# A hybrid attention and mixture-of-experts block on one core: the large weights are laid out by the host in blocks of 1 MiB, 8 KiB per partition

## The chip, the cores and the metric

The kernel runs on one core of one Trainium2 chip. The metric is the device time of one execution in microseconds (us), lower is better. The kernel before took 781.64 us as the median of three runs (780.91 to 783.07). Arithmetic that the host does on its side before the launch (sorting an input into another order in memory) is not part of this time; what the device reads and computes is.

## The reference

One decoder block over 256 tokens of 1024 channels, in float32. Two token mixers work on the same normed input, are gated, merged and projected; then each token goes to two of 32 experts.

```python
h = rmsnorm(x, g_mix); proj = h @ w_in            # w_in: 1024 x 7936
q_d, k_d, v_d, q_s, k_s, v_s, gate_d, gate_s = split_cols(proj, IN_WIDTHS)
y_dil = dilated_attention(q_d, k_d, v_d)          # 24 heads, three dilations
y_swa = swa_sink_attention(q_s, k_s, v_s, sinks)  # 16 query heads on 2 key heads
mixed = sigmoid(gate_d) * (y_dil @ w_br_dil) + sigmoid(gate_s) * (y_swa @ w_br_swa)
x = x + mixed @ w_out
# hier_moe(rmsnorm(x, g_ffn)): the best of 4 groups, the two best of its 8 experts
for e in range(32):
    a = silu(hf @ w_e_gate[e]) * (hf @ w_e_up[e])  # 1024 x 512 each
    out = out + gates[:, e:e + 1] * (a @ w_e_down[e])  # 512 x 1024
x = rmsnorm(x + out, g_final)
```

The weights are far larger than the data: w_in, w_br_dil, w_br_swa and w_out hold 43 MB, the three expert weights 32 x 6 MiB = 201 MB. All of them are read once.

## The kernel before

The work has two stages that overlap at their seam.

*The mixers* (to about 310 us). `Stream` (L153 to L172) brings the dense weights in tiles `w` of 128 partitions x 4 row blocks x 512 columns, 1 MiB each, in the order of the list `items`; four tiles rotate. A tile is asked for with one transfer, whose source is cut out of the weight matrix as it stands: for each partition four pieces of 512 neighbouring float32 (2 KiB), one from each of four rows of the matrix. `convert` (L232) splits each tile into two parts of lower precision with ScalarE (L248) and VectorE (L249), and TensorE multiplies both. A tile's slot is free for the next one once both engines have read it.

*The experts*. All 32 experts are computed for the tokens that chose them, 32 slots per expert. Their weights come in 192 chunks `ew` of 1 MiB, six per expert: four of gate and up (256 input rows each), two of down (256 hidden rows each). `fill` (L643) asks for them: a chunk of gate and up with two transfers of 512 KiB (one from `w_e_gate`, one from `w_e_up`), in which a partition gets two neighbouring rows of 512 float32 (4 KiB, in one piece); a chunk of down with one transfer of 1 MiB, two pieces of 4 KiB per partition from rows 128 apart. Chunks go into a ring of slots, which grows whenever the mixers give up a buffer (`release`); `prefetch` asks for the next chunk as soon as the program has come to a place where one is called for, and the chunk's slot has been read by TensorE. Per expert TensorE gathers tokens (`ga`, for four experts at a time), multiplies by gate and up (`gu`), turns the activation (`atp`), multiplies by down (`dn`) and adds into four accumulators (`quad`).

Nearly all transfers are issued by one queue, SyncE's (SP), in program order: a transfer whose slot is not free holds back all that stand behind it. The framework also gives each transfer one of eight completion semaphores in turn (DMAHW0 to DMAHW7 in the rows of the order below), and a transfer waits until the one that had the semaphore before has landed. So at most eight are under way.

The rows of an input channel and its place: in the gate and up chunks partition p holds rows 2p and 2p+1 of 256, so the transposes of x2 (`xtp`, L127 called from `route_piece`) and the gathers (`ga`) read x2 with a step of two elements; the router weights `wr` and the norm's gains `fcol` are stored the same way.

```python
src[(k0 + j) * P:(k0 + j + step) * P, c0:c0 + ncol].rearrange("(k p) c -> p k c", p=P),  # L170, dense tile
src[e, 256 * i:256 * (i + 1), :].rearrange("(p r) c -> p (r c)", r=2))                   # L648, gate or up
w_e_down[e, 256 * i + rows * j:256 * i + rows * (j + 1), :].rearrange("(c p) o -> p c o", p=P))  # L655, down
```

Of the kernel before, what the change touches and what calls it, by code (L numbers as in the profile page):

```python
# [9 lines left out]
F32 = mybir.dt.float32  # L10
# [74 lines left out]
def tile_hybrid_block(  # L85
    ctx: ExitStack,
    tc: tile.TileContext,
    x, g_mix, w_in, sinks, w_br_dil, w_br_swa, w_out, g_ffn, w_group, b_group,
    w_router, b_router, w_e_gate, w_e_up, w_e_down, g_final, c_small, c_big, out,
):  # L90
    nc = tc.nc
    x, w_in, out = x[0], w_in[0], out[0]
    w_br_dil, w_br_swa, w_out = w_br_dil[0], w_br_swa[0], w_out[0]
    w_group, w_router = w_group[0], w_router[0]
    w_e_gate, w_e_up, w_e_down = w_e_gate[0], w_e_up[0], w_e_down[0]
# [14 lines left out]
    # x and the output come with the tokens by their class, the token modulo 4, and in order within it:  # L110
    # place 64 c + j is token 4 j + c.
# [19 lines left out]
    # ---------------------------------------------------------------- loads  # L131
# [4 lines left out]
    frow = sb.tile([4, 2 * P], F32, tag="ct0", name="frow")  # L136
# [17 lines left out]
    class Stream:  # L154
        """Dense weights, 512 columns by 4 row blocks of 128, in the order they are used."""
# [4 lines left out]
        def load(self):  # L160
            if self.n >= len(self.items):
                return
            src, k0, nk, c0, ncol = self.items[self.n]
            s = self.free.pop(0)
            t = slot(s, [P, 4, 512], f"w{self.n}")
            step = 2 if self.n == 0 else nk
            for j in range(0, nk, step):
                SP.dma_start(
                    t[:, j:j + step, :ncol],
                    src[(k0 + j) * P:(k0 + j + step) * P, c0:c0 + ncol].rearrange("(k p) c -> p k c", p=P),  # L170
                )
            self.tiles[self.n] = (t, s)  # L172
            self.n += 1
# [4 lines left out]
    def unit(src, nk, c0, ncol, kind, arg=None):  # L178
        first = len(items)
        for k0 in range(0, nk, 4):  # L180
            items.append((src, k0, min(4, nk - k0), c0, ncol))
        units.append(dict(first=first, nk=nk, ncol=ncol, kind=kind, arg=arg))

    for g in (1, 2, 0):
        unit(w_in, 8, O_QD + 512 * g, 512, "qd", g)
        unit(w_in, 8, O_KD + 512 * g, 512, "kd", g)
        unit(w_in, 8, O_VD + 512 * g, 512, "vd", g)
    unit(w_in, 8, O_KS, 256, "kvs")
    for j in range(2):
        unit(w_in, 8, O_QS + 512 * j, 512, "qs", j)  # L190
    for j in range(2):
        unit(w_in, 8, O_GD + 512 * j, 512, "gd", j)
    for j in range(2):
        unit(w_in, 8, O_GS + 512 * j, 512, "gs", j)
    for j in range(2):
        unit(w_br_dil, 4, 512 * j, 512, "brd", j)
    for j in range(2):
        unit(w_br_swa, 8, 512 * j, 512, "brs", j)
    for j in range(2):
        unit(w_out, 8, 512 * j, 512, "out", j)  # L200
# [5 lines left out]
    SP.dma_start(frow, g_ffn[0].rearrange("(k c) -> k c", c=2 * P))  # L206
# [9 lines left out]
    wr = sb.tile([P, 4, 2, NG + NE], F32, tag="ct1", name="wr")  # L216
    with nc.allow_non_contiguous_dma(reason="router weights: rows of 16 and 128 bytes, once"):
        for k2 in range(4):
            SP.dma_start(
                wr[:, k2, :, 0:NG], w_group[k2 * 256:(k2 + 1) * 256, :].rearrange("(p r) c -> p r c", r=2))  # L220
            SP.dma_start(
                wr[:, k2, :, NG:], w_router[k2 * 256:(k2 + 1) * 256, :].rearrange("(p r) c -> p r c", r=2))
# [4 lines left out]
    # ---------------------------------------------------------------- splitting of dense weights  # L227
# [4 lines left out]
    def convert(order=lambda i: i):  # L232
        """Split the next two row blocks of a dense weight into two float32r parts, exactly."""
# [35 lines left out]
    # ---------------------------------------------------------------- h = rmsnorm(x), transposed, split  # L269
# [17 lines left out]
    fcol = sm("fcol", [P, 4, 2])  # L287
# [73 lines left out]
    def evac(un, half, o):  # L361
# [78 lines left out]
    def unit_steps(u):  # L440
        """One unit as steps of a row-block pair each: two passes over the same weights."""
# [116 lines left out]
    def dil_slot(i):  # L558
        """One head slot of the dilated attention: in the two wider groups a query's keys are of its class."""
# [36 lines left out]
    def pipelined(gens, parts):  # L596
        """Scores of one, transposes of the one before, values of the one before that."""
# [34 lines left out]
    # ---------------------------------------------------------------- expert weights  # L632
# [28 lines left out]
    def release(*slots):  # L661
        """These slots are free for expert weights from here on."""
# [14 lines left out]
    # ---------------------------------------------------------------- routing  # L677
# [12 lines left out]
    def route_piece(t, k):  # L690
        """256 columns of x2 of one token tile: squares summed, transposed for the logits."""
# [4 lines left out]
        for r in range(2):  # L696
            turn128(tp[:, r * P:(r + 1) * P], x2[:, t, k, r, :])
# [17 lines left out]
    def route_pick(t):  # L715
        """The first of the best groups, its two best experts, the pairs' places in line."""
# [34 lines left out]
    def route_gates(t):  # L751
        """Weights of the two: softmax of the group's maximum, times the pair's."""
# [15 lines left out]
    # ---------------------------------------------------------------- the mixers  # L768
# [10 lines left out]
    V.tensor_tensor(out=wr, in0=wr, in1=fcol.unsqueeze(3).to_broadcast([P, 4, 2, NG + NE]), op=ALU.mult)  # L779
# [8 lines left out]
    late["x2"] = x2 = late["x"].rearrange("p t (k c r) -> p t k r c", k=4, r=2)  # L788
# [23 lines left out]
    # how many came per expert; what lies beyond the slots  # L812
# [14 lines left out]
    # ---------------------------------------------------------------- experts  # L827
# [6 lines left out]
    def gather(e0):  # L834
        """Tokens of experts e0 .. e0+3 in their slots, transposed, normed."""
# [28 lines left out]
        if e0 == 0:  # L864
            # the first token tile is done while the second is still on its way
# [22 lines left out]
    def scatter_matrix(e):  # L888
        """One-hot slots by tokens of expert e, on each quarter of the partitions, and the slots' gates."""
# [18 lines left out]
    def gateup(e):  # L908
        """Gate and up products of expert e: hidden columns 128 j.. on quarter j of the partitions."""
# [57 lines left out]
    # ---------------------------------------------------------------- x + experts, final norm  # L967
# [160 lines left out]
```

## Time and profile before

| | |
|---|---|
| median of three runs | 781.64 us |
| span of the profiled execution, first to last instruction | 779.8 us |
| what lies around the span (median less span) | 1.84 us |
| TensorE busy | 674.3 us (86%) |
| VectorE, ScalarE busy | 294.6 us, 225.9 us |
| read by the DMA engines | 249.89 MB in 81054 packets |
| chain that ended last | TensorE 55%, DMA 38% |

The profiled execution has no time of its own other than its span; the difference to the median of the runs is taken as what lies around it. A packet in the profile is one piece that one of the 16 DMA engines moved; its size is the length of the run that is in one piece on both sides. The granted clock (PEclk) is 1.0 at 2.4 GHz and 0.5 at 1.2 GHz.

### The profile page before, as it was taken

How to read it: one execution, taken by the hardware profiler on the slowest of the kernel's cores; microseconds unless marked ns; L12 is line 12 of the kernel's file. 1: busy time of each engine (PE TensorE's matmuls, PEld its weight loads, DVE VectorE, ACT ScalarE, POOL GpSimd, SP SyncE). 2: the span in 40 equal slices, each digit the busy share in tenths (PEclk: the TensorE clock that was granted, in tenths of full speed). 3: DMA queues.
4: the chain of work that ended last, by engine and by line, in shares of the span. 5: the costliest groups of instructions: out<-in, count | busy, mean ns of one | idle time of the engine just before them, and what ended most of it. 6: DMA issues, size and time to landing. Idle time of an engine off the chain costs nothing.

```text
span 779.8 us, 15115 instructions
## 1 busy us (share of the span) xinstructions
PE 674.3 (86%) x6417; PEld 478.2 (61%) x6417; DVE 294.6 (38%) x749; ACT 225.9 (29%) x448; POOL 2.1 (0%) x10
## 2 busy tenths in 40 slices
PE   9999999999999999999987777878787787767682
PEld 8998988889788998765645334444434344433341
DVE  6564667874666675632222111211211111111102
ACT  5444575755677454310101000100000000000003
POOL 0000000000000000000000000000000000000000
PEclk9999999999999999999999679888978958987787
DMA  8786554336634778999999999999999999999993
GB/s 310 248 307 207 162 187 139 109 109 254 232 109 156 273 293 311 337 369 407 408 408 410 408 408 408 408 407 408 409 409 408 409 409 409 408 407 409 408 408 135
DMA packets 81054, 249.89 MB, mean 320 GB/s; under 512 B 8652, under 2 KB 10072, under 8 KB 80984
## 3 DMA queue, kind: packets, MB, share of 16 engines
q1 hardware_dynamic: 80824, 248.82, 83.5%
q8 instruction: 52, 0.85, 0.4%
q14 instruction: 18, 0.15, 0.1%
q10 hardware_dynamic: 160, 0.07, 0.0%
HBM read 247.82 MB, written 1.05 MB: 319 GB/s over the span
## 4 chain that ended last, share of the span: by engine, by line
PE 55%; DMA 38%; DVE 3%; ACT 2%; issue 1%; SPq 0%; ACTq 0%; DVEq 0%
PE acc L121 29%; DMA ew<-in_w_e_up_dram 17%; DMA ew<-in_w_e_down_dram 11%; DMA ew<-in_w_e_gate_dram 10%; PE gu L121 7%; PE quad L121 7%; PE dn L121 4%; PE ga L121 3%; PE dpv L121 1%; PE ct L899 1%; PE spv L121 1%; PE dtp L579 1%; PE stp L542 1%; PE ct L121 1%; PE atp L127 1%
## 5 line engine op out<-in xcount | busy, mean ns | idle before, releaser
L121 PE MATMUL gu<-ew,xes 128*32 128x256 f32 x2048 | 153.7, 416 | 36.9 <-DMA ew<-in_w_e_up_dram 36.9
L121 PE MATMUL acc<-hT_hi,wh 128*128 128x256 f32 x800 | 147.7, 285 | 0.8 <-DVE qa L401 0.8
L121 PEld LDWEIGHTS acc<-hT_hi,wh 128*128 128x128 f32 x800 | 122.0, 188 | 4.4 <-issue 1.5
L121 PEld LDWEIGHTS gu<-ew,xes 128*32 128x32 f32 x2048 | 64.9, 116 | 93.8 <-issue 64.0
L249 DVE TENSOR_TENSOR wh<-w,wh 128x1024 fp32r<-128x1024 f32 (+1 forms) x84 | 100.2, 1198 | 44.3 <-ACT wh L248 42.7
L121 PE MATMUL acc<-hT_lo,wh 128*128 128x256 f32 x400 | 111.4, 279 | 0.0
L248 ACT CAST wh<-w 128x1024 fp32r<-128x1024 f32 (+1 forms) x84 | 86.1, 1028 | 49.7 <-PE acc L121 42.9
L121 PE MATMUL dn<-ew,ws 128*32 128x256 f32 x1024 | 84.8, 468 | 3.5 <-DMA ew<-in_w_e_down_dram 2.8
L925 DVE TENSOR_TENSOR ws<-ws,gu 128x128 f32<-128x128 f32 x32 | 9.2, 286 | 194.0 <-ACT ws L922 194.0
L121 PEld LDWEIGHTS acc<-hT_lo,wh 128*128 128x128 f32 x400 | 75.1, 188 | 0.4 <-issue 0.4
L922 ACT ACTIVATE ws<-gu 128x128 f32<-128x128 f32 x32 | 8.9, 278 | 215.1 <-PE gu L121 215.1
L121 PEld LDWEIGHTS dn<-ew,ws 128*32 128x32 f32 x1024 | 33.1, 128 | 33.2 <-issue 12.8
L951 ACT ACTIVATE y_hi<-dn,gsl 128x256 fp32r<-128x256 f32 x32 | 15.2, 474 | 114.5 <-PE dn L121 114.5
L121 PE MATMUL ga<-ws,x_again 128*128 128x128 f32 x256 | 39.3, 315 | 4.8 <-DVE ws L938 3.8
L121 PEld LDWEIGHTS ga<-ws,x_again 128*128 128x128 f32 x256 | 36.0, 221 | 8.9 <-DVE ws L938 6.9
L953 DVE SCALAR_TENSOR_TENSOR y_lo<-dn,gsl,y_hi 128x256 fp32r<-128x256 f32 x32 | 15.5, 483 | 66.6 <-ACT y_hi L951 66.6
L121 PE MATMUL quad<-y_hi,cts 32*128 32x256 f32 x256 | 24.0, 361 | 15.0 <-ACT y_hi L951 15.0
L121 PEld LDWEIGHTS quad<-y_hi,cts 32*128 32x128 f32 x256 | 14.2, 208 | 33.3 <-ACT y_hi L951 32.1
L121 PE MATMUL quad<-y_lo,cts 32*128 32x256 f32 x256 | 32.6, 392 | 2.3
L860 ACT ACTIVATE xes<-ga,fcol 128x128 f32<-128x128 f32 x32 | 11.7, 368 | 79.0 <-DVE xes L862 79.0
L892 DVE TENSOR_SCALAR ws<-cs,pos 128x128 f32<-128x128 f32 x64 | 17.8, 281 | 41.6 <-PE ct L121 41.6
L121 PEld LDWEIGHTS quad<-y_lo,cts 32*128 32x128 f32 x256 | 19.0, 205 | 21.9 <-issue 14.3
(199 smaller groups left out, 769.0 us busy)
## 6 DMA issues: line engine op xcount, KB each, us to landing
ew<-in_w_e_gate_dram SPq DMA_DIRECT2D x128, 512.0 KB, 12.7
ew<-in_w_e_up_dram SPq DMA_DIRECT2D x128, 512.0 KB, 12.8
ew<-in_w_e_down_dram SPq DMA_DIRECT2D x63, 1024.0 KB, 12.7
w<-in_w_in_dram SPq DMA_DIRECT2D x29, 1024.0 KB, 5.2
w<-in_w_br_swa_dram SPq DMA_DIRECT2D x4, 1024.0 KB, 5.2
w<-in_w_out_dram SPq DMA_DIRECT2D x4, 1024.0 KB, 6.6
w<-in_w_in_dram SPq DMA_DIRECT2D x4, 512.0 KB, 5.8
w<-in_w_br_dil_dram SPq DMA_DIRECT2D x2, 1024.0 KB, 5.2
```

The source lines that it names most:

```text
L121: i = PE.matmul(o, lhsT, rhs, start=start, stop=stop, skip_group_check=True)
L127: i = PE.transpose(o, src, ident)
L248: order(A.copy(w[:, 0, :, :ncol], r))
L249: order(V.tensor_tensor(out=w[:, 1, :, :ncol], in0=r, in1=w[:, 0, :, :ncol].bitcast(F32), op=ALU.subtract))
L542: PE.transpose(tp[:, j * P:(j + 1) * P], pp[:, 384 * b + j * P:384 * b + (j + 1) * P], ident)
L579: PE.transpose(tp[:, h * P:(h + 1) * P], pp[:, 384 * h + j * P:384 * h + (j + 1) * P], ident)
L860: A.activation(dst, src, AF.Copy, scale=col)
L892: eq = V.tensor_scalar(dd[:, t, :].rearrange("p (g s) -> p g s", g=REP), cs[:, C_CNT:C_CNT + CAP].unsqueeze(1).to_broadcast([P, REP, CAP]) ...
L922: A.activation(ac, gu[:, 0:P], AF.Silu)
L925: V.tensor_tensor(out=ac, in0=ac, in1=gu[:, P:2 * P], op=ALU.mult)
L951: A.activation(y_hi, dn[:, 0:256], AF.Copy, scale=gsl)
L953: V.scalar_tensor_tensor(out=y_lo, in0=dn[:, 0:256], scalar=gsl, in1=y_hi.bitcast(F32), op0=ALU.mult, op1=ALU.subtract)
```

## The change

The host writes each large weight into memory in the order in which the kernel reads it: a block of 1 MiB per transfer, in it the partitions one after the other, 8 KiB each. The dense tiles and the chunks of the experts keep their sizes and their places in SBUF. Gate and up of a chunk stand side by side in one block and come with one transfer in place of two. A partition's rows in these chunks are now p and p+128 of 256, so x2, `wr` and `fcol` are read without the step of two, and the one transpose that makes `fcol` replaces two (L319). The narrow tile of the shared keys and values (`kvs`, 256 columns) gets a block of its own, with pieces of 1 KiB as before. The first dense tile is still asked for in two halves, as is the last chunk of down: there a piece is 4 KiB.

```diff
-            src, k0, nk, c0, ncol = self.items[self.n]
+            src, nk, ncol = self.items[self.n]
             s = self.free.pop(0)
             t = slot(s, [P, 4, 512], f"w{self.n}")
             step = 2 if self.n == 0 else nk
             for j in range(0, nk, step):
-                SP.dma_start(
-                    t[:, j:j + step, :ncol],
-                    src[(k0 + j) * P:(k0 + j + step) * P, c0:c0 + ncol].rearrange("(k p) c -> p k c", p=P),
-                )
+                SP.dma_start(t[:, j:j + step, :ncol], src[:, j:j + step, :])
...
-            items.append((src, k0, min(4, nk - k0), c0, ncol))
+            items.append((src[k0 // 4], 4, ncol))
...
-        unit(w_in, 8, O_QD + 512 * g, 512, "qd", g)
+        unit(w_in[g], 8, 512, "qd", g)
...
     fps = bank("T", [P, 512], "fps")
-    for r in range(2):
-        PE.transpose(fps[:, 4 * r:4 + 4 * r], frow[:, r::2], ident[0:4, 0:4])
-    V.tensor_copy(fcol.rearrange("p k r -> p r k"), fps[:, 0:8].rearrange("p (r k) -> p r k", r=2))
+    PE.transpose(fps[:, 0:8], frow, ident[0:8, 0:8])
+    V.tensor_copy(fcol, fps[:, 0:8])
...
     def fill(t, e, what, i):
         if what == 0:
-            for j, src in enumerate((w_e_gate, w_e_up)):
-                SP.dma_start(
-                    t[:, j * 1024:(j + 1) * 1024],
-                    src[e, 256 * i:256 * (i + 1), :].rearrange("(p r) c -> p (r c)", r=2))
+            SP.dma_start(t, w_e_gu[e, i].rearrange("p u r c -> p (u r c)"))
         else:
             parts = 2 if (e, i) == (NE - 1, 1) else 1
-            rows = 256 // parts
+            n = 2 // parts
             for j in range(parts):
                 SP.dma_start(
-                    t[:, 2048 // parts * j:2048 // parts * (j + 1)].rearrange("p (c o) -> p c o", o=D),
-                    w_e_down[e, 256 * i + rows * j:256 * i + rows * (j + 1), :].rearrange("(c p) o -> p c o", p=P))
+                    t[:, 1024 * n * j:1024 * n * (j + 1)],
+                    w_e_down[e, i, :, n * j:n * (j + 1), :].rearrange("p c o -> p (c o)"))
...
-            turn128(tp[:, r * P:(r + 1) * P], x2[:, t, k, r, :])
+            turn128(tp[:, r * P:(r + 1) * P], x2[:, t, 2 * k + r, :])
...
-    late["x2"] = x2 = late["x"].rearrange("p t (k c r) -> p t k r c", k=4, r=2)
+    late["x2"] = x2 = late["x"].rearrange("p t (k c) -> p t k c", k=NK)
...
-                mm(g[:, j * P:(j + 1) * P], x2[:, t, kr // 2, kr % 2, :], dp[:, t, :], t == 0 and j == 0, t == NT - 1)
+                mm(g[:, j * P:(j + 1) * P], x2[:, t, kr, :], dp[:, t, :], t == 0 and j == 0, t == NT - 1)
...
+def _blocks(w):
+
+    k, c = w.shape
+    return w.reshape(k // 512, 4, P, c // 512, 512).transpose(3, 0, 2, 1, 4)
...
+    gu = np.stack([a["w_e_gate"][0], a["w_e_up"][0]], axis=1)
+    a["w_e_gu"] = gu.reshape(NE, 2, 4, 2, P, HID).transpose(0, 2, 4, 1, 3, 5)
+    a["w_e_down"] = a["w_e_down"][0].reshape(NE, 2, 2, P, D).transpose(0, 1, 3, 2, 4)
```

The order of the instructions on TensorE, VectorE, ScalarE and GpSimd stays as it was (but for the one transpose). On SP it changes in form. The first place is the start of the program: after the two halves of x the first dense tile in two halves (x2) and three more tiles. Before:

```order
L168 DMA w_87<-in_w_in_dram 128x2x512 x2
L168 DMA w_90<-in_w_in_dram 128x4x512
L168 DMA w_92<-in_w_in_dram 128x4x512
L168 DMA w_94<-in_w_in_dram 128x4x512
L205 DMA cs<-c_small_dram 128x208
```

and of the change:

```order
L167 DMA w_87<-in_w_in_dram 128x1024 x2
L167 DMA w_90<-in_w_in_dram 128x2048
L167 DMA w_92<-in_w_in_dram 128x2048
L167 DMA w_94<-in_w_in_dram 128x2048
L201 DMA cs<-c_small_dram 128x208
```

Nothing is moved here; the shape of the source is one run per partition (2048 elements) in place of four of 512. The second place is in the middle of the experts, the ten transfers of one expert before (gate and up of four chunks, two of down; `ew` is the chunk, DMAHW the semaphore of the transfer eight before, PE the slot's last reader):

```order
L646 DMA ew_3395<-in_w_e_gate_dram 128x1024 [waits DMAHW0_49,PE_49]
L646 DMA ew_3395<-in_w_e_up_dram 128x1024 [waits DMAHW1_49]
L646 DMA ew_3398<-in_w_e_gate_dram 128x1024 [waits DMAHW2_49,PE_49]
L646 DMA ew_3398<-in_w_e_up_dram 128x1024 [waits DMAHW3_49]
L646 DMA ew_3401<-in_w_e_gate_dram 128x1024 [waits DMAHW4_49,PE_49]
L646 DMA ew_3401<-in_w_e_up_dram 128x1024 [waits DMAHW5_49]
L646 DMA ew_3404<-in_w_e_gate_dram 128x1024 [waits DMAHW6_49,PE_49]
L646 DMA ew_3404<-in_w_e_up_dram 128x1024 [waits DMAHW7_49]
L653 DMA ew_3459<-in_w_e_down_dram 128x2x1024 [waits DMAHW0_49,PE_49]
L653 DMA ew_3461<-in_w_e_down_dram 128x2x1024 [waits DMAHW1_49,PE_49]
```

and the same expert after, with the two chunks that follow:

```order
L639 DMA ew_3378<-in_w_e_gu_dram 128x2048 [waits DMAHW0_49,PE_49]
L639 DMA ew_3380<-in_w_e_gu_dram 128x2048 [waits DMAHW1_49,PE_49]
L639 DMA ew_3382<-in_w_e_gu_dram 128x2048 [waits DMAHW2_49,PE_49]
L639 DMA ew_3384<-in_w_e_gu_dram 128x2048 [waits DMAHW3_49,PE_49]
L644 DMA ew_3438<-in_w_e_down_dram 128x2048 [waits DMAHW4_49,PE_49]
L644 DMA ew_3440<-in_w_e_down_dram 128x2048 [waits DMAHW5_49,PE_49]
L639 DMA ew_3493<-in_w_e_gu_dram 128x2048 [waits DMAHW6_49]
L639 DMA ew_3495<-in_w_e_gu_dram 128x2048 [waits DMAHW7_49]
```

Six transfers per expert stand where ten stood, in the same order of chunks, and the eight semaphores now span eight MiB where they spanned four or five MiB.

## Rows read from the trace of the kernel before

**Rows 1.** The page's part 2: 40 equal slices; granted clock in tenths, GB/s moved.
```profile
PEclk9999999999999999999999679888978958987787
...
GB/s 310 248 307 207 162 187 139 109 109 254 232 109 156 273 293 311 337 369 407 408 408 410 408 408 408 408 407 408 409 409 408 409 409 409 408 407 409 408 408 135
```

**Rows 2.** Windows: per engine busy us (instructions); granted clock, DMA share, GB/s.
```profile
0.00:300.00 300.00, 296.35 (x2204) 263.01 (x2205) 192.41 (x385) 172.79 (x305) 0.32 (x6) 1.00 0.61 210
300.00:346.00 46.00, 44.51 (x409) 33.26 (x411) 25.09 (x98) 13.54 (x34) 1.83 (x4) 1.00 0.88 326
346.00:760.00 414.00, 327.49 (x3741) 179.09 (x3733) 71.44 (x252) 31.84 (x85) 0.00 (x0) 0.86 1.03 408
```

**Rows 3.** Waits of SP's queue: us in total, times, longest us.
```profile
SPq L168 <- DVE wh L249: 152.1, 27, 14.0
SPq L646 <- DMA ew<-in_w_e_down_dram: 116.4, 53, 2.8
```

**Rows 4.** Chain that ended last, its end: start us, us, what.
```profile
754.65 11.69 DMA ew<-in_w_e_down_dram
766.38 0.68 PE dn L121 x8
```

**Rows 5.** DMA from 346 to 760 us: packets, queues, issues (KB, us to landing).
```profile
DMA packets 45467, 169.03 MB, mean 408 GB/s; under 512 B 4300, under 2 KB 4300, under 8 KB 45430
...
q8 instruction: 30, 0.49, 0.5%
...
ew<-in_w_e_down_dram SPq DMA_DIRECT2D x53, 1024.0 KB, 12.7
```

**Rows 6.** DMA from 30 to 42 us, dense tiles alone.
```profile
DMA packets 2338, 4.67 MB, mean 389 GB/s; under 512 B 66, under 2 KB 66, under 8 KB 2337
```

**Rows 7.** Windows where the stream of transfers last has gaps.
```profile
338.00:340.00 2.00, 2.00 (x31) 1.01 (x24) 0.77 (x4) 1.08 (x3) 0.00 (x0) 1.00 0.67 193
...
342.00:344.00 2.00, 2.00 (x29) 0.97 (x22) 0.74 (x4) 0.00 (x0) 0.00 (x0) 1.00 0.92 305
```

**Rows 8.** SP's issues in one expert's time: start us, us, what.
```profile
456.19 0.33 SPq L646 DMA_DIRECT2D ew<-in_w_e_up_dram  x1
...
466.42 0.33 SPq L646 DMA_DIRECT2D ew<-in_w_e_up_dram  x1
469.05 0.33 SPq L646 DMA_DIRECT2D ew<-in_w_e_gate_dram  x1
471.56 0.33 SPq L646 DMA_DIRECT2D ew<-in_w_e_up_dram  x1
```

**Rows 9.** Waits, whole span (first row) and to 310 us (second).
```profile
PE gu L121 <- DMA ew<-in_w_e_up_dram: 36.9, 35, 2.8
...
ACT wh L248 <- DMA w<-in_w_in_dram: 2.6, 2, 1.9
```

**Rows 10.** TensorE's weight loads by form: busy us, mean ns, idle before.
```profile
L542 PEld LDWEIGHTS stp<-cs,pps 128*128 128x128 f32 x48 | 5.5, 140 | 0.4 <-ACT pT L359 0.2
...
L127 PEld LDWEIGHTS xtp<-cs,x_again 128*128 128x128 f32 x16 | 2.8, 216 | 0.2
```

**Rows 11.** TensorE's timeline at the granted clocks 1.0 and 0.5 (last row).
```profile
395.74 2.80 PE L121 MATMUL gu<-ew,xes 128*32 128x256 f32 x48
...
400.68 1.93 PE L121 MATMUL dn<-ew,ws 128*32 128x256 f32 x32
...
405.64 2.80 PE L121 MATMUL gu<-ew,xes 128*32 128x256 f32 x48
...
418.47 2.80 PE L121 MATMUL gu<-ew,xes 128*32 128x256 f32 x48
...
440.76 3.64 PE L121 MATMUL dn<-ew,ws 128*32 128x256 f32 x32
```

**Rows 12.** Windows at the end of the stream of transfers.
```profile
760.00:761.00 1.00, 0.23 (x3) 0.03 (x1) 0.00 (x0) 0.00 (x0) 0.00 (x0) 1.00 0.97 389
...
766.00:767.00 1.00, 0.62 (x8) 0.16 (x8) 0.00 (x0) 0.00 (x0) 0.00 (x0) 1.00 0.39 143
```

More of the change, by code (lines that the diff above doesn't have):

```diff
@@ L87, in tile_hybrid_block @@
     tc: tile.TileContext,
-    x, g_mix, w_in, sinks, w_br_dil, w_br_swa, w_out, g_ffn, w_group, b_group,
-    w_router, b_router, w_e_gate, w_e_up, w_e_down, g_final, c_small, c_big, out,
+    x, g_mix, w_in, w_kvs, sinks, w_br_dil, w_br_swa, w_out, g_ffn, w_group, b_group,
+    w_router, b_router, w_e_gu, w_e_down, g_final, c_small, c_big, out,
 ):
     nc = tc.nc
-    x, w_in, out = x[0], w_in[0], out[0]
-    w_br_dil, w_br_swa, w_out = w_br_dil[0], w_br_swa[0], w_out[0]
+    x, out = x[0], out[0]
     w_group, w_router = w_group[0], w_router[0]
-    w_e_gate, w_e_up, w_e_down = w_e_gate[0], w_e_up[0], w_e_down[0]
     sb = ctx.enter_context(tc.tile_pool(name="sb", bufs=1))
@@ L135, in tile_hybrid_block @@
     grow = sb.tile([8, P], F32, tag="ct1", name="grow")
-    frow = sb.tile([4, 2 * P], F32, tag="ct0", name="frow")
+    frow = sb.tile([8, P], F32, tag="ct0", name="frow")
     SP.dma_start(xt[:, 0, :], x[0:P])
@@ L176, in tile_hybrid_block, with unit @@
     items = []
-    def unit(src, nk, c0, ncol, kind, arg=None):
+    def unit(src, nk, ncol, kind, arg=None):
         first = len(items)
         for k0 in range(0, nk, 4):
-            items.append((src, k0, min(4, nk - k0), c0, ncol))
+            items.append((src[k0 // 4], 4, ncol))
         units.append(dict(first=first, nk=nk, ncol=ncol, kind=kind, arg=arg))
     for g in (1, 2, 0):
-        unit(w_in, 8, O_QD + 512 * g, 512, "qd", g)
-        unit(w_in, 8, O_KD + 512 * g, 512, "kd", g)
-        unit(w_in, 8, O_VD + 512 * g, 512, "vd", g)
-    unit(w_in, 8, O_KS, 256, "kvs")
+        unit(w_in[g], 8, 512, "qd", g)
+        unit(w_in[3 + g], 8, 512, "kd", g)
+        unit(w_in[6 + g], 8, 512, "vd", g)
+    unit(w_kvs[0], 8, 256, "kvs")
     for j in range(2):
-        unit(w_in, 8, O_QS + 512 * j, 512, "qs", j)
+        unit(w_in[9 + j], 8, 512, "qs", j)
     for j in range(2):
-        unit(w_in, 8, O_GD + 512 * j, 512, "gd", j)
+        unit(w_in[11 + j], 8, 512, "gd", j)
     for j in range(2):
-        unit(w_in, 8, O_GS + 512 * j, 512, "gs", j)
+        unit(w_in[13 + j], 8, 512, "gs", j)
     for j in range(2):
-        unit(w_br_dil, 4, 512 * j, 512, "brd", j)
+        unit(w_br_dil[j], 4, 512, "brd", j)
     for j in range(2):
-        unit(w_br_swa, 8, 512 * j, 512, "brs", j)
+        unit(w_br_swa[j], 8, 512, "brs", j)
     for j in range(2):
-        unit(w_out, 8, 512 * j, 512, "out", j)
+        unit(w_out[j], 8, 512, "out", j)
     stream = Stream(items)
@@ L205, in tile_hybrid_block @@
     SP.dma_start(cs[:, P:], c_small[:, P:])
-    SP.dma_start(frow, g_ffn[0].rearrange("(k c) -> k c", c=2 * P))
+    SP.dma_start(frow, g_ffn[0].rearrange("(k c) -> k c", c=P))
     cb = slot(9, [P, C_DIL], "cb")
@@ L215, in tile_hybrid_block @@
     SP.dma_start(sink, sinks[0:1, :].to_broadcast([P, 16]))
-    wr = sb.tile([P, 4, 2, NG + NE], F32, tag="ct1", name="wr")
+    wr = sb.tile([P, NK, NG + NE], F32, tag="ct1", name="wr")
     with nc.allow_non_contiguous_dma(reason="router weights: rows of 16 and 128 bytes, once"):
         for k2 in range(4):
-            SP.dma_start(
-                wr[:, k2, :, 0:NG], w_group[k2 * 256:(k2 + 1) * 256, :].rearrange("(p r) c -> p r c", r=2))
-            SP.dma_start(
-                wr[:, k2, :, NG:], w_router[k2 * 256:(k2 + 1) * 256, :].rearrange("(p r) c -> p r c", r=2))
+            rows = slice(k2 * 256, (k2 + 1) * 256)
+            SP.dma_start(wr[:, 2 * k2:2 * k2 + 2, 0:NG], w_group[rows, :].rearrange("(r p) c -> p r c", r=2))
+            SP.dma_start(wr[:, 2 * k2:2 * k2 + 2, NG:], w_router[rows, :].rearrange("(r p) c -> p r c", r=2))
     rb = sb.tile([P, NG + NE], F32, tag="rb", name="rb")
@@ L286, in tile_hybrid_block @@
     gcol = sm("gcol", [P, 8])
-    fcol = sm("fcol", [P, 4, 2])
+    fcol = sm("fcol", [P, NK])
     for t in range(NT):
@@ L707, in route_logits @@
         for r in range(2):
-            rt["last"] = mm(quad[t][:, 0:NG + NE], xT[:, r * P:(r + 1) * P], wr[:, k, r, :],
+            rt["last"] = mm(quad[t][:, 0:NG + NE], xT[:, r * P:(r + 1) * P], wr[:, 2 * k + r, :],
                             k + r == 0, k + r == 4)
@@ L778, in tile_hybrid_block @@
     late["ys_lo"] = slot(5, [P, 8, T], "ys_lo", F32R)
-    V.tensor_tensor(out=wr, in0=wr, in1=fcol.unsqueeze(3).to_broadcast([P, 4, 2, NG + NE]), op=ALU.mult)
+    V.tensor_tensor(out=wr, in0=wr, in1=fcol.unsqueeze(2).to_broadcast([P, NK, NG + NE]), op=ALU.mult)
     interleave(steps_of(("gs", "brd")), pipelined((swa_pair(a) for a in range(8)), 2), 32.0 / 23.0)
@@ L852, in products @@
                 kr = 4 * hh + j
-                mm(g[:, j * P:(j + 1) * P], x2[:, t, kr // 2, kr % 2, :], dp[:, t, :], t == 0 and j == 0, t == NT - 1)
+                mm(g[:, j * P:(j + 1) * P], x2[:, t, kr, :], dp[:, t, :], t == 0 and j == 0, t == NT - 1)
         def normed(g, hh):
             for j in range(4):
-                col = fcol[:, 2 * hh + j // 2, j % 2:j % 2 + 1]
+                col = fcol[:, 4 * hh + j:4 * hh + j + 1]
                 dst, src = xe[:, hh * 512 + j * P:hh * 512 + (j + 1) * P], g[:, j * P:(j + 1) * P]
@@ L1001, in general @@
                 for t in range(NT):
-                    mm(o[:, t * P:(t + 1) * P], x2[:, t, kr // 2, kr % 2, :], dg[:, t * P:(t + 1) * P], True, True)
-                V.tensor_scalar(h2T[:, kr * T:(kr + 1) * T], o[:, 0:T], fcol[:, kr // 2, kr % 2:kr % 2 + 1], None,
-                                op0=ALU.mult)
+                    mm(o[:, t * P:(t + 1) * P], x2[:, t, kr, :], dg[:, t * P:(t + 1) * P], True, True)
+                V.tensor_scalar(h2T[:, kr * T:(kr + 1) * T], o[:, 0:T], fcol[:, kr:kr + 1], None, op0=ALU.mult)
             wgv = wg.rearrange("p (u k r c) -> p u k r c", u=2, k=4, r=2)
@@ L1011, in general @@
                         wd.rearrange("p (c o) -> p c o", c=2),
-                        w_e_down[bass.ds(e, 1), 256 * i:256 * (i + 1), :].rearrange("a (c p) o -> p (a c) o", p=P))
+                        w_e_down[bass.ds(e, 1), i].rearrange("a p c o -> p (a c) o"))
                 for j in range(4):
-                    for u, src in enumerate((w_e_gate, w_e_up)):
+                    for u in range(2):
                         for k2 in range(4):
@@ L1017, in general @@
                                 wgv[:, u, k2],
-                                src[bass.ds(e, 1), 256 * k2:256 * (k2 + 1), j * P:(j + 1) * P].rearrange(
-                                    "a (p r) c -> p (a r) c", r=2))
+                                w_e_gu[bass.ds(e, 1), k2, :, u, :, j * P:(j + 1) * P].rearrange(
+                                    "a p r c -> p (a r) c"))
                     o = bank("T", [P, 512], f"og{j}")
@@ L1094, in tile_hybrid_block, with _laid_out @@
     general(*tiles)
-_INS = ["x", "g_mix", "w_in", "sinks", "w_br_dil", "w_br_swa", "w_out", "g_ffn", "w_group", "b_group",
-        "w_router", "b_router", "w_e_gate", "w_e_up", "w_e_down", "g_final"]
+_INS = ["x", "g_mix", "w_in", "w_kvs", "sinks", "w_br_dil", "w_br_swa", "w_out", "g_ffn", "w_group", "b_group",
+        "w_router", "b_router", "w_e_gu", "w_e_down", "g_final"]
+def _blocks(w):
+    k, c = w.shape
+    return w.reshape(k // 512, 4, P, c // 512, 512).transpose(3, 0, 2, 1, 4)
+def _laid_out(inputs):
+    a = {name: np.asarray(v) for name, v in inputs.items()}
+    n, d = a["x"].shape[1:]
+    a["x"] = a["x"].reshape(n // 4, 4, d).transpose(1, 0, 2).reshape(1, n, d)
+    w = a["w_in"][0]
+    a["w_in"] = _blocks(np.concatenate([w[:, :O_KS], w[:, O_GD:]], axis=1))
+    a["w_kvs"] = w[:, O_KS:O_GD].reshape(1, 2, 4, P, 256).transpose(0, 1, 3, 2, 4)
+    for name in ("w_br_dil", "w_br_swa", "w_out"):
+        a[name] = _blocks(a[name][0])
+    gu = np.stack([a["w_e_gate"][0], a["w_e_up"][0]], axis=1)
+    a["w_e_gu"] = gu.reshape(NE, 2, 4, 2, P, HID).transpose(0, 2, 4, 1, 3, 5)
+    a["w_e_down"] = a["w_e_down"][0].reshape(NE, 2, 2, P, D).transpose(0, 1, 3, 2, 4)
+    return a
 def kernel(**inputs):
@@ L1113 @@
     n, d = inputs["x"].shape[1:]
+    laid_out = _laid_out(inputs)
     for name in _INS:
-        a = inputs[name]
-        if name == "x":
-            a = np.asarray(a).reshape(n // 4, 4, d).transpose(1, 0, 2).reshape(1, n, d)
-        given(f"in_{name}_dram", a)
+        given(f"in_{name}_dram", laid_out[name])
     small, big = _constants()
```

1 line of the change is left out of this document (removed).

## The prediction, made before the changed kernel had run

> **What bounds the kernel now.** I first read the slices of the page: from slice 18 on (351 us) the line GB/s stands at 407 to 410 until the last slice, and nothing before it is so flat [rows 1]. The windows by stage say the same in one line each [rows 2]. To 300 us TensorE is busy 296.35 of 300 us at the full granted clock, and the transfers fill 0.61 of their engines: TensorE bounds the mixers. From 346 to 760 us TensorE is busy 327.49 of 414 us at a mean granted clock of 0.86, and the transfers fill 1.03: they bound the experts. Next the waits of SP's queue, to see what a transfer waits for: in the mixers for a slot (152.1 us on VectorE's split of the tile), in the experts for the landing of the transfer eight before it (116.4 us in one row) and hardly ever for TensorE [rows 3]. So there is always a queue of eight, and the time of a transfer is set by how fast the engines move bytes. Last the end of the chain: the last chunk of down lands at 766.34 (754.65 + 11.69) and TensorE begins on it at 766.38 [rows 4]; what follows to 779.8 is 13.4 us of the last expert, the norm and the store, which the change does not touch.
>
> **The change part by part.**
>
> *Longer runs.* What does a run's length cost? Two stretches in which the engines are full answer it. From 346 to 760 us there are 45467 packets, of which 4300 are tiny and 37 are 8 KB or more; the other 41130 times 4096 bytes is 168.5 of the 169.03 MB, so the chunks came in runs of 4 KB, at 408 GB/s [rows 5]. From 30 to 42 us there are 2338 less 66 = 2272, times 2048 bytes = 4.65 of 4.67 MB: dense tiles in runs of 2 KB, at 389 GB/s [rows 6]. One of 16 engines then spends 16 x 2048 / 389 = 84.2 ns on a run of 2 KB and 16 x 4096 / 408 = 160.6 ns on one of 4 KB. The second 2 KB cost 76.4 ns, so 7.8 ns of a run do not depend on its length. The trace has no run of 8 KB on this queue. By the straight line it takes 7.8 + 4 x 76.4 = 313.4 ns, which is 16 x 8192 / 313.4 = 418.2 GB/s (an estimate from these two rows). The bounds: nothing is gained beyond 4 KB (408), or the fixed part goes altogether (16 x 2048 / 76.4 = 428.9 GB/s). A loss is not excluded, since the new addresses are another pattern (below, among the rivals). I take the line, 418.2.
>
> *Where that counts.* The last gaps in the stream are at 338 to 344 us, 193 and 305 GB/s [rows 7]; from there to 760 us it is full. A stretch bound by bytes shrinks by 1 - 408/418.2 = 2.44%: of the 414 us 10.1, and of the ramp before and the drain after (8 us and 6 us) 0.3. That is 10.4 us. Per expert it is 15.37 us (471.56 - 456.19 [rows 8]) becoming 15.0.
>
> *Longer runs in the dense tiles* (2 KB to 8 KB, 389 to 418). Hidden under TensorE, which is busy 296.35 of the first 300 us [rows 2]; the split waits twice for a dense tile, 2.6 us in all [rows 9], while TensorE has products of the tiles before. The first tile's halves become runs of 4 KB: 524288 bytes at 408 in place of 389 is 0.06 us sooner. I take 0; the bounds are 0 and 2.6.
>
> *One transfer in place of two for gate and up.* 128 transfers go. A transfer is issued when the one eight before has landed, so the steps between issues are the steps between landings. After the issue at 456.19 eight halves land by 466.42, 10.23 us for 4 MiB, 2.56 per MiB; then two whole ones by 471.56, 5.14 us, 2.57 per MiB [rows 8]. Two halves cost no more than one whole; I take 0, from the nearest rows there are, for the merge. The Trainium skill speaks the other way: by "DMA: Bandwidth & Descriptors" (Bandwidth, Measured, its rule) transfers should be gathered to 1 MiB or more, and the same page's anatomy of a transfer puts a fixed cost of about 2.0 us on each. The trace does not agree as long as eight are under way; what the rule would give stands among the rivals.
>
> *More under way.* The eight semaphores now hold 8.4 MB where they held 12.7 us x 408 GB/s = 5.2 MB [rows 5]. A chunk is issued earlier and lands 8.4 / 418.2, some 20 us, after its issue. It lands in the same order, so this alone moves nothing.
>
> *Reading x2 without a step.* The transposes that read x2 in steps of two load 128 columns in 216 ns, those of the attention without a step in 140 [rows 10]. Sixteen of them lie at 300 to 325 us, on TensorE's path to the experts: at most 16 x 76 ns = 1.2 us, at least 0, since a weight load runs beside the product before it. That stretch releases slots and so starts the full stream. I take 0.3, nearer to 0, as TensorE is never seen idle after such a load. The 256 loads of the gathers lie where the transfers bound, and one transpose less for fcol lies beside TensorE's first products: 0.
>
> *What is late next.* TensorE. At the full clock an expert takes 9.90 us (the wait for the activation included) and one with half a gather 12.83 (405.64 - 395.74 and 418.47 - 405.64 [rows 11]). With two of four of each that is 11.4, below 15.0. What hides it stays, though at the half clock the products of down take 3.64 in place of 1.93 us [rows 11].
>
> *Sum.* 10.4 + 0.3 = 10.7 us off the span of 779.8 is 769.1. The median of the runs stands 1.84 us above that span; with the same around it, 770.9 us.
>
> **The rivals.**
>
> *Nothing beyond 4 KB.* A run of 8 KB goes as two of 4 KB, or as one at the same rate. For it: no run on this queue was longer than 4 KB, so the line is drawn from two points outwards. Against: other queues of this trace moved 30 packets with 0.49 MB, 16 KB each [rows 5], so an engine does take longer pieces. Time: 781.6 less 0.3, 781.3. The Trainium skill bears on it, against this change: "DMA: Bandwidth & Descriptors" (SWDGE vs HWDGE vs iDMA) gives a packet preferably at most 4096 B. By that the sum is 781.3; whether the limit holds on SP's queue no row here shows.
>
> *A loss: the engines drift apart.* At the end of the stream the rate falls from 389 GB/s at 760 to 143 at 766 to 767 us [rows 12]: the engines that are done first are some 5.8 us ahead of those that land the last chunk. If that lead grows with what is under way, 5.8 x 8.4 / 5.2 = 9.4, the last chunk lands 3.6 us later. With no gain in rate: 785.2. It is slower from the point where the rate stays below 411 GB/s (3.6 of 428 us is 0.8% of 408). For it: nothing but the semaphores ties the engines together. Against: 5.8 us is less than the 12.7 that were under way, so the lead was not what the queue allowed.
>
> *TensorE takes over.* If it stays at the half clock, where its work nearly doubles, 11.4 us per expert would be about 21, above 15.0; then slots come free late and half of the gain may go: 776. For it: the mean clock of 0.86. Against: it waits 36.9 us for chunks of gate and up [rows 9], more than three times the gain, and when it falls behind it has no waits and its clock was full (the first 80 us of the experts, slices 18 to 21 [rows 1]).
>
> *The fixed part goes altogether*, 428.9 GB/s: 428 us x (1 - 408/428.9) = 20.9 us, 760.5.
>
> *A fixed cost per transfer.* If each of the 128 transfers taken away had one, the halves in rows 8 would land slower per MiB than the wholes, and by those rows the gain is nothing. Time by rows: as forecast. By the skill's 2.0 us, eight under way at once, it would be 128 x 2.0 / 8 = 32 us more, an estimate from the page named above.
>
> **How the numbers follow.** A measurement of this kernel tells some 0.3% (2.3 us) from no change. Forecast (a rate of 412 to 425 GB/s): 0.72. The fixed part gone: 0.05. A fixed cost per transfer: 0.01. TensorE takes over: 0.04. All these are faster: 0.82. Nothing beyond 4 KB: 0.10, no change. A loss by drift or a worse pattern of addresses: 0.08, slower. The range begins at 764 (a rate of 425: 428 x 0.040 = 17.1, and the 0.3 of x2, off 781.6) and reaches to 782.5, which takes in no gain; outside are most of the loss and the far end of the gain, some 0.15.
>
> **What would show it.** Right: the stream from 346 us on flat at about 418 GB/s in packets of 8 KB, half as many; 15.0 us between the issues of one expert; transfers landing about 20 us after issue; the first 300 us as before to within a microsecond; still 13 us from the last landing to the end. Wrong: packets of 4 KB, or 408 GB/s in packets of 8 KB (the line does not go on); a drop longer than 6 us at the end of the stream (drift); waits of SP for TensorE, and no waits of TensorE for chunks (TensorE takes over); a gain that comes before 346 us.

## The result, and the profile after

The changed kernel takes 769.07 us (median of four runs, 768.40 to 770.38), the kernel before beside it 781.54 us; the ratio is 0.984 with a 95% interval of 0.9824 to 0.9856. The forecast was 770.9 us: a gain of 10.7 where 12.5 were measured. The profiled execution is the run of 768.40 us with a span of 766.6 us; 1.8 us lie around the span, as before.

The page's slices first, beside [rows 1] of before:

```profile
span 766.6 us, 14858 instructions
...
PEclk9999999999999999999998979879977977988787
...
GB/s 316 286 285 203 165 173 157 112 111 221 273 62 153 281 330 306 297 365 419 421 418 418 421 420 419 421 420 421 418 420 422 418 420 422 420 419 421 420 418 127
DMA packets 39333, 249.87 MB, mean 326 GB/s; under 512 B 6608, under 2 KB 8032, under 8 KB 9824
```

The flat stretch still begins at slice 18, now at 418 to 422 GB/s, and it still ends in the last slice. The span is 13.2 us shorter, with as many bytes in half the packets. The same stages as in [rows 2] (busy us and number of instructions of PE, PEld, DVE, ACT and POOL, then granted clock, DMA share, GB/s):

```profile
0.00:300.00 300.00, 295.96 (x2206) 262.76 (x2207) 193.10 (x385) 173.55 (x306) 0.32 (x6) 1.00 0.58 212
300.00:346.00 46.00, 44.39 (x427) 32.63 (x428) 25.26 (x100) 13.59 (x36) 1.81 (x4) 1.00 0.87 336
346.00:747.00 401.00, 316.30 (x3719) 170.32 (x3712) 70.91 (x248) 31.16 (x84) 0.00 (x0) 0.88 1.01 420
```

To 300 us TensorE's line reads as before (295.96 us busy against 296.35). From 346 us on the rate is 420 where 408 stood, while the granted clock (0.88 for 0.86) and the engines' share (1.01 for 1.03) hardly moved. From 300 to 346 us it is 336 GB/s where 326 stood; what that is worth stands further down. The transfers from 346 to 745 us, the line that answers [rows 5]:

```profile
DMA packets 22989, 167.49 MB, mean 420 GB/s; under 512 B 2548, under 2 KB 2548, under 8 KB 2599
...
ew<-in_w_e_gu_dram SPq DMA_DIRECT2D x104, 1024.0 KB, 19.8
ew<-in_w_e_down_dram SPq DMA_DIRECT2D x52, 1024.0 KB, 19.9
```

22989 packets less the 2599 under 8 KB are 20390, and 20390 x 8192 bytes are 167.0 of the 167.49 MB: the chunks come in pieces of 8 KB. A transfer lands 19.8 us after its issue, where it took 12.7. SP's issues [rows 8] are merged here, as nothing waits between two of a kind (start, us, what):

```profile
459.09 2.83 SPq L644 DMA_DIRECT2D ew<-in_w_e_down_dram  x2
464.06 7.79 SPq L639 DMA_DIRECT2D ew<-in_w_e_gu_dram  x4
474.00 2.81 SPq L644 DMA_DIRECT2D ew<-in_w_e_down_dram  x2
479.21 7.79 SPq L639 DMA_DIRECT2D ew<-in_w_e_gu_dram  x4
```

From the first issue of down to the next expert's it is 474.00 - 459.09 = 14.91 us, from one block of gate and up to the next 15.15: about 15.0 us per expert, where 15.37 stood. SP waits for slots of the dense tiles first and then for landings, as before (us in total, times, longest):

```profile
SPq L167 <- DVE wh L244: 152.0, 26, 14.1
SPq L644 <- DMA ew<-in_w_e_gu_dram: 111.2, 52, 3.3
SPq L639 <- DMA ew<-in_w_e_down_dram: 106.5, 50, 3.5
```

and TensorE for chunks, 33.7 us in place of the 36.9 of [rows 9]:

```profile
PE gu L119 <- DMA ew<-in_w_e_gu_dram: 33.7, 34, 2.6
```

The end of the chain, for [rows 4]:

```profile
735.93 17.40 DMA ew<-in_w_e_down_dram
...
753.37 0.68 PE dn L119 x8
```

The last chunk lands at 753.33 (735.93 + 17.40); to 766.6 there are 13.3 us, as the 13.4 of before. And the drain of the stream, for [rows 12]:

```profile
746.00:747.00 1.00, 1.00 (x17) 0.42 (x17) 0.00 (x0) 0.00 (x0) 0.00 (x0) 1.00 1.01 414
747.00:748.00 1.00, 0.51 (x3) 0.31 (x3) 0.00 (x0) 0.00 (x0) 0.00 (x0) 1.00 0.87 344
748.00:749.00 1.00, 0.62 (x12) 0.42 (x16) 0.00 (x0) 0.00 (x0) 0.00 (x0) 1.00 0.59 229
...
753.00:754.00 1.00, 0.63 (x8) 0.16 (x8) 0.00 (x0) 0.00 (x0) 0.00 (x0) 1.00 0.27 111
```

The rate drops within 747 to 748 us, runs at about half from 748 on, and 111 GB/s are left at 753 to 754: some 6 us again, with more bytes under way than before.

### The profile page after: what moved, and what is told of

It reads as the page before. It is cut to its first block, busy times and chain, and to the rows that moved or that the text cites. A ratio compares the mean times of both kernels' runs of the same rounds, so it can differ in the third digit from the quotient of the medians.

```text
span 766.6 us, 14858 instructions
## 1 busy us (share of the span) xinstructions
PE 662.8 (86%) x6416; PEld 468.8 (61%) x6416; DVE 294.9 (38%) x749; ACT 226.0 (29%) x448; POOL 2.1 (0%) x10
## 4 chain that ended last, share of the span: by engine, by line
DMA 50%; PE 45%; DVE 2%; ACT 1%; issue 1%; SPq 0%; DVEq 0%; ACTq 0%
DMA ew<-in_w_e_gu_dram 31%; PE acc L119 29%; DMA ew<-in_w_e_down_dram 18%; PE quad L119 5%; PE gu L119 3%; PE dn L119 1%; PE dpv L119 1%; PE spv L119 1%; PE ga L119 1%; PE dtp L573 1%; PE stp L536 1%; DMA xt<-in_x_dram 1%; DVE wh L244 0%; DVE ks L369 0%; PE ct L890 0%
## 5 line engine op out<-in xcount | busy, mean ns | idle before, releaser
L119 PE MATMUL gu<-ew,xes 128*32 128x256 f32 x2048 | 152.5, 413 | 33.8 <-DMA ew<-in_w_e_gu_dram 33.7
L119 PEld LDWEIGHTS gu<-ew,xes 128*32 128x32 f32 x2048 | 61.7, 116 | 92.6 <-DMA ew<-in_w_e_gu_dram 48.8
L119 PE MATMUL dn<-ew,ws 128*32 128x256 f32 x1024 | 81.8, 457 | 2.4 <-DMA ew<-in_w_e_down_dram 1.7
L119 PE MATMUL ga<-ws,x_again 128*128 128x128 f32 x256 | 34.2, 289 | 4.8 <-DVE ws L929 3.8
L119 PEld LDWEIGHTS ga<-ws,x_again 128*128 128x128 f32 x256 | 31.2, 199 | 8.7 <-DVE ws L929 6.7
L851 ACT ACTIVATE xes<-ga,fcol 128x128 f32<-128x128 f32 x32 | 11.6, 367 | 73.8 <-DVE xes L853 73.8
L119 PEld LDWEIGHTS quad<-y_lo,cts 32*128 32x128 f32 x256 | 18.5, 200 | 21.6 <-issue 13.9
## 6 DMA issues: line engine op xcount, KB each, us to landing
ew<-in_w_e_gu_dram SPq DMA_DIRECT2D x128, 1024.0 KB, 19.8
ew<-in_w_e_down_dram SPq DMA_DIRECT2D x63, 1024.0 KB, 19.8
```

The source lines that it names most:

```text
L119: i = PE.matmul(o, lhsT, rhs, start=start, stop=stop, skip_group_check=True)
L851: A.activation(dst, src, AF.Copy, scale=col)
```

## The experiments

The theory on trial: an engine pays a fixed time per run (a run is a stretch of bytes in one piece) beside the time per byte, and the gain comes from that. Its rivals: fewer and larger transfers, the order of addresses, the dense tiles, and the reading of x2.

**e3_run4k: large transfers, short runs.** The block of a chunk is laid out in two halves, so that a partition's 8 KB are two runs. The chunks of down are changed in the same way, which the excerpt leaves out.

```diff
-            SP.dma_start(t, w_e_gu[e, i].rearrange("p u r c -> p (u r c)"))
+            SP.dma_start(t.rearrange("p (u x) -> p u x", u=2), w_e_gu[e, i].rearrange("u p r c -> p u (r c)"))
...
-    a["w_e_gu"] = gu.reshape(NE, 2, 4, 2, P, HID).transpose(0, 2, 4, 1, 3, 5)
+    a["w_e_gu"] = gu.reshape(NE, 2, 4, 2, P, HID).transpose(0, 2, 1, 4, 3, 5)
```

Expected: 

> The changed kernel with one thing taken back in the expert weights: each chunk is one transfer of 1 MiB out of one block of 1 MiB, six per expert, but a partition's 8 KB come as two runs of 4 KB that lie 512 KiB apart in the block. Theory 'the length of the run sets the rate': 408 GB/s from 346 us on, 428 us x (420/408 - 1) = 12.6 us slower than the changed kernel less nothing, 780.5 to 781.5 us. Rival 'fewer and larger transfers, eight MiB under way, give the gain': 420 GB/s and 769 us with packets of 4 KB.

Measured: 780.36 us, ratio to the kernel before 0.9991 (0.9981 to 1.0001). From 346 to 740 us, windows and then packets:

```profile
346.00:740.00 394.00, 309.45 (x3555) 166.27 (x3551) 69.13 (x243) 30.35 (x81) 0.00 (x0) 0.86 1.03 408
```
```profile
DMA packets 41644, 160.95 MB, mean 408 GB/s; under 512 B 2443, under 2 KB 2443, under 8 KB 41610
```

The rate is back at 408. One transfer of 1 MiB per chunk, blocks in order of address, six transfers per expert and 18.5 us from issue to landing (19.8 in the changed kernel) are all still there, and they give nothing that these runs can tell from no change. SP waits more often here for slots that TensorE has yet to read, so a little less is under way: 18.5 us x 408 GB/s = 7.5 MB. That is not what sets the rate, as the kernel before moved 408 GB/s with 5.2 MB under way. The rival of fewer and larger transfers falls.

**e4_run2k: the same with four runs of 2 KB.** As the diff above, with four pieces of 512 float32 per partition in gate and up and in down.

Expected: 

> As the kernel before this one in the list, with runs of 2 KB (four per partition, 256 KiB apart in the block): still one transfer of 1 MiB per chunk out of one block in order. Theory 'a fixed 7.8 ns per run beside 76.4 ns per 2 KB, whatever the addresses': 389 GB/s, 15.42 x 408/389 = 16.2 us per expert, some 20 us slower than with runs of 4 KB, 801 us. Rival 'the dense tiles ran at 389 because they were cut out of a wide matrix': above 400 GB/s and under 790 us, as the pieces lie side by side here.

Measured: 805.24 us, ratio 1.031 (1.0293 to 1.0327).

```profile
346.00:740.00 394.00, 305.79 (x3384) 162.34 (x3377) 66.70 (x236) 29.50 (x79) 0.00 (x0) 0.82 1.05 386
```
```profile
DMA packets 76407, 152.18 MB, mean 386 GB/s; under 512 B 2311, under 2 KB 2311, under 8 KB 76375
```

The experts' stream runs at 386 GB/s out of blocks that lie in order: the rate that the dense tiles had when cut out of wide matrices. 801 us were expected from 389; the kernel is 4 us slower than that, and its rate 3 GB/s lower.

**m1_runs: the transfers alone.** A kernel of its own with one stage for each length of run:

```python
stage("r1", 1, 1, total=16)
stage("r2", 2, 1)
stage("r2m", 2, 1, pitch=True)      # cut out of w_in
stage("r4", 4, 1)
stage("r8", 8, 1)
stage("r8h", 8, 1, halves=True)     # two transfers of 64 partitions
stage("r16", 16, 2)
stage("r32", 32, 4)
```

Expected: 

> Transfers alone, nothing is computed and the output is left at zero: eight stages, each drained before the next, of 24 MiB of the expert weights (16 in the first), eight transfers under way: runs of 1 KB, 2 KB, 2 KB cut out of the matrix w_in (rows of 31 KB), 4 KB, 8 KB in transfers of 1 MiB, 8 KB in transfers of 512 KiB (64 partitions each), 16 KB in 2 MiB, 32 KB in 4 MiB. Theory 'a fixed time per run and engine, by the rows of before and after 8 to 9 ns': in the full part of each stage some 350 GB/s at 1 KB, 389 at 2 KB in both layouts, 408 at 4 KB, 419 at 8 KB in both sizes of transfer, 425 at 16 KB, 428 at 32 KB. Rival 'the size of the transfer': 8 KB in 512 KiB slower than in 1 MiB, and 4 KB in 1 MiB as fast as 8 KB. Rival 'the address pattern': the two stages with 2 KB apart, the block faster. Rival 'a ceiling near 420': 16 and 32 KB no faster than 8 KB.

Measured, the full part of each stage in that order (busy us of DVE and POOL, granted clock, DMA share, GB/s):

```profile
8.00:48.00 40.00, 0.00 (x0) 0.00 (x0) 1.00 1.10 349
60.00:114.00 54.00, 0.00 (x0) 0.00 (x0) 1.00 1.05 388
124.00:184.00 60.00, 0.00 (x0) 0.00 (x0) 1.00 1.05 388
192.00:248.00 56.00, 0.00 (x0) 0.00 (x0) 1.00 1.03 410
256.00:310.00 54.00, 0.00 (x0) 0.00 (x0) 1.00 1.01 423
320.00:424.00 104.00, 0.00 (x0) 0.00 (x0) 1.00 1.02 220
436.00:490.00 54.00, 0.00 (x0) 0.00 (x0) 1.00 1.01 430
498.00:550.00 52.00, 0.00 (x0) 0.00 (x0) 1.00 1.00 433
```

The packets of the fifth stage show that a run of 8 KB goes as one:

```profile
DMA packets 3141, 22.85 MB, mean 423 GB/s; under 512 B 352, under 2 KB 352, under 8 KB 352
```

(3141 - 352) x 8192 bytes are all 22.85 MB. In ns of one of 16 engines per run (16 x length / rate): 46.9, 84.5, 84.5, 159.8, 309.9, then 609.7 and 1210.8. From 1 KB on each further KB costs 37.5 to 37.7 ns, over five doublings, and some 9 ns are left over for the run itself (9.4 by the first two stages). Scattered and ordered runs of 2 KB agree to 388 GB/s: the rival of the addresses falls too. A ceiling near 420 is not there: 16 and 32 KB go on to 430 and 433, though these two stages also have larger transfers. The sixth stage, 8 KB in transfers of 512 KiB, is far off this line, at 220 GB/s. By the sign that was set down for it this speaks for the rival of the size, but its transfers also have only 64 partitions; with 128 partitions, transfers of 512 KiB moved 408 GB/s in the kernel before, and 4 KB in 1 MiB is not as fast as 8 KB (410 against 423).

**e1_step2: x2 read in steps of two again.** The router weights and the gains are stored to match, which the excerpt leaves out; all else is as in the changed kernel.

```diff
-    late["x2"] = x2 = late["x"].rearrange("p t (k c) -> p t k c", k=NK)
+    late["x2"] = x2 = late["x"].rearrange("p t (k c r) -> p t k r c", k=4, r=2)
...
-    a["w_e_gu"] = gu.reshape(NE, 2, 4, 2, P, HID).transpose(0, 2, 4, 1, 3, 5)
+    a["w_e_gu"] = gu.reshape(NE, 2, 4, P, 2, HID).transpose(0, 2, 3, 1, 4, 5)
```

Expected: 

> The changed kernel with one part undone: inside a block of gate and up the rows of a partition are 2p and 2p+1 again, and x2, the router weights and the gains are read in steps of two as before; runs of 8 KB and one transfer per chunk stay. Theory 'the step costs TensorE time before the stream is full': the stretch from 302 to 322 us is 0.2 us longer than in the changed kernel, the gathers 2.15 in place of 2.05 us, the whole 0.4 to 1.0 us slower (769.5 to 770.1 us). Rival 'the step costs nothing, the last microsecond is the rate too': the same as the changed kernel, 769.1 us, within 0.3.

Measured: 769.91 us, ratio to the kernel before 0.9866 (0.985 to 0.9883). TensorE's first transpose of x2, second and fourth gather, in the changed kernel

```profile
302.00 0.38 PE L125 MATMUL xtp<-cs,x_again 128*128 128x128 f32 x2
...
321.73 2.05 PE L119 MATMUL ga<-ws,x_again 128*128 128x128 f32 x16 [0.93 <-DVE ws L839]
...
342.48 2.05 PE L119 MATMUL ga<-ws,x_again 128*128 128x128 f32 x16
```

and with the step:

```profile
302.80 0.39 PE L125 MATMUL xtp<-cs,x_again 128*128 128x128 f32 x2
...
322.74 2.15 PE L119 MATMUL ga<-ws,x_again 128*128 128x128 f32 x16 [0.93 <-DVE ws L840]
...
343.68 1.56 PE L119 MATMUL ga<-ws,x_again 128*128 128x128 f32 x11
```

The last row is cut at 345 us, where the window ends; its start counts here. From the first transpose to the second gather 19.73 us against 19.94, to the fourth 40.48 against 40.88: the step costs 0.2 and 0.4 us there. The load of the transposes, changed kernel first, shows where (busy us, mean ns, idle before):

```profile
L125 PEld LDWEIGHTS xtp<-cs,x_again 128*128 128x128 f32 x16 | 2.1, 156 | 0.4
```
```profile
L125 PEld LDWEIGHTS xtp<-cs,x_again 128*128 128x128 f32 x16 | 2.8, 216 | 0.2
```

**e2_dense_old: the dense tiles as before**, the experts in blocks.

```diff
-                SP.dma_start(t[:, j:j + step, :ncol], src[:, j:j + step, :])
+                SP.dma_start(
+                    t[:, j:j + step, :ncol],
+                    src[(k0 + j) * P:(k0 + j + step) * P, c0:c0 + ncol].rearrange("(k p) c -> p k c", p=P),
+                )
```

Expected: 

> The changed kernel with the dense weights as before: tiles of 1 MiB cut out of the matrices in runs of 2 KB, only the expert weights in blocks of 8 KB per partition. Theory 'only the experts' stream counts': 769.1 us, at most 0.6 us more (what TensorE was earlier at 302 us). Rival 'the dense tiles give part of the gain, as they share the engines with the chunks fetched ahead': 2 to 3 us of the 12.5 are lost, 771 to 772 us.

Measured: 769.96 us, ratio 0.986 (0.9843 to 0.9876). The rival's 771 to 772 us did not come. As this kernel and the one before it came out 0.8 us above the changed kernel, which had run at another time, all three ran once more beside each other.

**c1_after, c2_step2, c3_dense_old.** The changed kernel unaltered, with the step, and with the old dense tiles.

Expected: 

> The changed kernel unaltered, beside the next two on one chip, since the runs with one part undone came 0.8 us slower than it in another sitting. 769 to 770 us.

Expected: 

> The changed kernel with the step of two in x2 kept, again. Theory 'the step costs 0.2 us from the first transpose of x2 to the second gather and 0.4 us to the fourth, and that is all': 0.2 to 0.4 us above the run before it. Rival 'the step costs the whole 0.8 us seen': 0.8 us above.

Expected: 

> The changed kernel with the dense weights in runs of 2 KB, again. Theory 'the mixers are TensorE's and nothing of the gain is theirs': as the changed kernel within 0.3 us. Rival 'the 0.6 us that TensorE was earlier at 302 us in one profile are the dense tiles': 0.6 to 0.8 us above.

Measured: 769.14 us (768.68 to 770.30), 769.82 us (769.18 to 770.30) and 769.11 us (768.11 to 770.63); ratios to the kernel before 0.9843 (0.983 to 0.9857), 0.9851 (0.9837 to 0.9864) and 0.9842 (0.9827 to 0.9857). With the old dense tiles the median is 0.03 us lower, so the runs show no worth of the new ones. As single runs spread over 1.1 to 2.5 us, they alone can't exclude the 0.6 to 0.8 us of the rival. The trace speaks against it: the first transpose of x2, at 302.00 us in the changed kernel's first profile and 301.75 in that of c1, comes at 301.56 with the old tiles. The profile of c3 has the dense tiles in runs of 2 KB again (from 30 to 42 us):

```profile
DMA packets 2323, 4.63 MB, mean 386 GB/s; under 512 B 71, under 2 KB 71, under 8 KB 2322
```

The step of x2 comes out 0.7 us dearer, within the spread of single runs; the traces give 0.4, and whether the other 0.3 are real stays open.

## Why the prediction was right, point by point

*What bounds the kernel* was read rightly: nearly all of the gain lies where the transfers are full. The prediction named a gain before 346 us as a sign of being wrong, and the traces show a small one. Up to 346 us 78.10 MB had been moved before and 78.96 MB after, which is 2.1 us of the stream at 408 GB/s. It does not come from the longer runs of the experts, as e3 had moved 78.99 MB by then with runs of 4 KB. Part of it is scatter between executions: the kernel with the old dense tiles had moved 78.59 MB in one (e2) and 79.01 MB in another (c3), and its first transpose of x2 came at 302.72 and 301.56 us, on both sides of the 302.00 of the changed kernel. The medians of several runs tell the worth better. e3 has all of the change but the longer runs of the experts, and it is 0.8 us faster than the kernel before, with an interval from 0.1 us slower to 1.5 us faster.

*Longer runs.* The step of the sum that carried all, a straight line from 2 and 4 KB out to 8 KB, held: 420 GB/s against the 418.2 forecast. From 346 to 740 us the traces have 160.89 MB before and 165.39 after, 408.4 and 419.8 GB/s, by which the same term reads 428 x (1 - 408.4/419.8) = 11.6 us in place of 10.4. With the 0.8 us of e3 for all that is not the length of the experts' runs that makes 12.4, and 12.5 were measured. So the mechanism was right and a size was off. The part that was mis-sized is the fixed time, 7.8 ns per run; the long stages of the transfers alone give 9.4. It came out low because the 389 GB/s of [rows 6] were a little high. The 12 us of that row hold the beginning of a burst, with 398 GB/s in the first 2 us and 387 in the other 10, and longer stretches of 2 KB run at 386 to 388 (e4, m1). With 386 the same working gives 9.2 ns and 420 GB/s.

*Dense tiles* 0, and *one transfer for two* 0: the runs show nothing against either (c3 and e3). On the second the Trainium skill, "DMA: Bandwidth & Descriptors" (Bandwidth), asks for transfers of 1 MiB or more, beside a table measured on transfers that GpSimd issues. On SP's queue with eight under way the trace does not agree that it matters at 512 KiB, as 408 GB/s were there with six transfers per expert and with ten.

*x2 without a step*, 0.3: the traces show 0.2 to 0.4. Only part of that is the transposes. Each of the first four gathers, which lie before the stream is full, takes 0.1 us less, and the prediction had put all gathers where the transfers bound.

*More under way*: landings after 19.8 us (20 were said), order and drain unchanged. That it moves nothing by itself is shown only within the 0.8 us of e3, in which it stands together with the merged transfers and x2.

*What is late next*: TensorE did not take over. It waits 33.7 us for chunks, nearly what it did (24.9 in c3 and 38.6 in c1), at a granted clock of 0.88 where it was 0.86.

The rivals: nothing beyond 4 KB is refuted by packets of 8 KB at 420 GB/s, and in m1_runs 688 pieces of 32 KB, 22.5 MB, went as one each. The 4096 B that the Trainium skill's "DMA: Bandwidth & Descriptors" (SWDGE vs HWDGE vs iDMA) prefers for a packet stand there for transfers that GpSimd issues; as a limit on the pieces of SP's queue these runs do not bear them out. The drift is refuted by a drain of the same 6 us with 20 us of transfers under way. The fixed part is not gone at 8 KB: it is paid once per run, so it weighs half as much per byte as at 4 KB.

## What to carry to other kernels

Where a stretch is bound by transfers, look at the bytes per packet first: here an engine paid about 9 ns per run beside 37.5 ns per KB (m1_runs), so that going from 4 to 8 KB is worth 3%, from 2 to 8 KB 9%, and from 8 to 16 KB 1.7% more. Two saturated stretches with different runs in one trace were enough to work out a third length to within 2 GB/s; a longer stretch of 2 KB would have come closer. What the gain is worth in the end is read from the stage: the same edit on the dense weights, under a busy TensorE, gave nothing.

## What was not expected

Runs of 8 KB in transfers of 64 partitions each, two for a block, moved 220 GB/s, little more than half of the 423 of the same block in one transfer of 128 partitions. The share of the DMA engines read 1.02 and 1.01, so each piece took about twice as long (16 x 8192 / 220 = 596 ns); a full share is no proof of a full rate. The Trainium skill's "DMA: Bandwidth & Descriptors" (Rules for kernel authors) says of such halves only that they do not pay, as they share the same engines. Why they cost half was not tried.

Open: runs of 16 KB in the kernel itself. They moved 430 GB/s in m1_runs, where 8 KB moved 423 and the kernel's stream 420; so some 427 GB/s are an estimate for that stream. But they need pairs of neighbouring slots, which the kernel's buffers, shared with the mixers, don't offer; it was not tried. Nor was it settled why about half of the rate is gone in the last 6 us of the stream, before and after; the stages of m1_runs do not show a drain of that length.
